# Opening an attention stream earlier in a two-block fp32 stack: buffers after the query and key projections, and 12 of 40 steps among the first fronts and value projections

## The chip, the cores and the metric

The kernel runs on one core of one Trainium2 chip. The metric is the device time of one execution in microseconds (us). TensorE is called PE here (PEld is its weight load), VectorE DVE, ScalarE ACT, and SP is the engine whose queue issues nearly all of the DMAs. Each engine works through its own list of instructions in order and waits in place when an operand or a buffer is not ready.

## What is computed

Two transformer blocks on 256 latent tokens and 256 context tokens of width 1024, all in float32. The second block has two layers, and its first layer mixes the tokens with `even_mixer`, which joins a grouped-query attention (8 heads, 2 key/value heads) with a two-directional RWKV-7 scan (8 heads):

```python
def even_mixer(h_lat, h_ctx, ...):
    p_lat = h_lat @ w_in
    p_ctx = h_ctx @ w_in
    ...
    oa_lat, oa_ctx = global_gqa(apply_rope(q_l, cos, sin), apply_rope(k_l, cos, sin), v_l,
                                q_c, k_c, v_c, ctx_out)
    f_lat = rwkv7_features(p_lat[..., A_COLS:], mu, w0, w2, a0, a2, g2, k_k, k_a)
    f_ctx = rwkv7_features(p_ctx[..., A_COLS:], mu, w0, w2, a0, a2, g2, k_k, k_a)
    ob_lat, ob_ctx = rwkv7_bidir(f_lat, f_ctx, r_k, gn_w, gn_b, ctx_out)
    o_lat = jnp.concatenate([oa_lat, ob_lat], axis=-1) @ w_out
```

The attention's result and the scan's result meet only in the output projection `w_out`. The attention needs the query and key/value projections; the scan needs the projections of r, k, v and of the decay, rate and gate vectors.

## The kernel before

Large products are split into a high and a low part and done as three matmuls (`mm3`, profile lines L113 to L115), so PE has three times the work of one product, and weights are cast on ACT (`whi`) and DVE (`wlo`) as they arrive.

`even_mixer` takes its projections and the first preparations of the scan in the order of the list `GA`: `q0` (queries), `r0` to `r3` (r and k of the scan), `k0` (keys and values of the attention), and then a mixture of `f` (the "front" of a unit of the scan), `b` (its "back"), `s` (its triangular solve) and `v0` to `v3` (the value projections). A unit of the scan is one direction of one block of 128 tokens; there are eight, numbered in the order of use. A front (L1461 on) makes the decays: `sg`, `eo`, `ei`, `ak`. A back makes `ar`, `bk` and the masked products `g` (L1540, with L1555 for the transposes), and stores a part of them to DRAM as `dq`. The solve (L1566) loads `dq` as `dl`, does 28 small DVE operations (`dt`, `dl`) one after the other, and stores `dy`. `do_k` and `do_q` store keys and queries to DRAM as `kd` and `qd`; `do_v` transposes its projection in the PSUM tag `tr` and stores it as `vd` (`stage`).

When the list is done, the pools of the projections are closed and `rwkv` begins. It goes through the units in four passes of two units each: `rwkv_maps` (products `m` with `x`, `T`, `lw`, `am`; L1609 to L1663) and then two scan steps (`rwkv_step`, products `y`, L1681 and L1690). Between the items of a pass it sets pieces of backs, solves and fronts of later units (`ahead_of`), pieces of gates and readout (`side`), and one step of the attention (`fill(FP)`, with `FP = 1`).

The attention (`even_attention`, `gqa`) is a generator of 40 steps: 8 pieces of 5 steps. The first four pieces use the first key/value head, the others the second; of each four, two have 512 keys (called big here: scores `sc` of 128x512 a head) and two have 256 (small: 128x256). The four heads of a piece each take a score (two matmuls into `sc`, L1001), a row maximum on DVE (L1003), an exponential on ACT (L1004), a reciprocal on DVE (L1005), a scaling by turns on ACT and DVE, transposes (`tr`, L1019) and a copy into `gpt`; the fifth step multiplies with the values (L1047) and stores to DRAM (`oTd`). A new piece puts two scores at its first step. The tag `sc` has one PSUM bank and so has `tr`, so that a score waits until the exponential of the one before has read its bank. Before, the generator is made at the start of `rwkv`, with a pool `at` of its own that is opened there, and its loads (`vv`, `K` of the first key/value head, `qS`) are issued at its first step; `K` has one buffer, so that the second load waits for the last score of the first four pieces.

What follows `rwkv` is `mixed`: output projection, with the stored attention output loaded as `orel`. Its first weight is `raw<-in_even_out`.

Of the kernel before, what the change touches and what calls it, by code (L numbers as in the profile page):

```python
# [45 lines left out]
def kernel(ctx: ExitStack, tc: tile.TileContext, A: dict, out: bass.AP, taps=None):  # L46
# [9 lines left out]
    def nm(s):  # L56
        uid[0] += 1
        return f"{s}_{uid[0]}"
# [58 lines left out]
    def tt(o, a, b, op):  # L117
        V.tensor_tensor(out=o, in0=a, in1=b, op=op)  # L118
# [101 lines left out]
    def acopy(d, s):  # L220
        S.copy(out=d, in_=s)
# [847 lines left out]
    def even_mixer(l, en):  # L1069
        T = 512  # L1070
        close_psum()
        with tc.tile_pool(name=nm("em"), bufs=1) as pk, tc.tile_pool(name=nm("rf"), bufs=2) as fp, \
# [59 lines left out]
            close_x()  # L1132
            held = [tc.tile_pool(name=nm("ru"), bufs=2), tc.tile_pool(name=nm("rs"), bufs=1)]
            C["up"], C["us"] = [held[0].__enter__(), None], held[1].__enter__()
            with tc.tile_pool(name=nm("ga"), bufs=1) as ga, tc.tile_pool(name=nm("emw"), bufs=2) as wk:
                zt = ga.tile([128, 260], F32, tag="zt", name="zt")
                V.memset(zt, 0.0)
                for x in dy:
                    nc.sync.dma_start(out=x.rearrange("l (a x) -> l a x", a=4), in_=zt[0:64].unsqueeze(1).to_broadcast([64, 4, 260]))
                K = ga.tile([128, 4, 512], F32R, tag="K", name="K0")  # L1140
                vv = ga.tile([128, 4, 128], F32, tag="vv", name="vv0")
                ropec = const("ropec", ga)
                rows = const("rows_g", ga)
                hsel = const("hsel", ga)
                tab = ga.tile([128, 2, 2, 2, 64], F32, tag="tab", name="tab")
                for gi in range(2):
                    g = rows[:, gi * 64:(gi + 1) * 64]
                    for t in range(2):
                        tt(tab[:, gi, t, 0], ropec[:, t, 0], g, ALU.mult)
                        g2 = g.rearrange("p (d s) -> p d s", s=2)  # L1150
                        z2 = tab[:, gi, t, 1].rearrange("p (d s) -> p d s", s=2)
                        r2 = ropec[:, t, 1].rearrange("p (d s) -> p d s", s=2)
                        for a in range(2):
                            tt(z2[:, :, a], r2[:, :, a], g2[:, :, 1 - a], ALU.mult)

                def stage(dst, n, srcs):
                    o = wk.tile([128, 4, 128], F32, tag="st", name=nm("st"), bufs=1)
                    transpose4(o[:, :n], srcs, lambda o, s: acopy(o, s.rearrange("p (j t) -> p j t", j=n)))
                    nc.sync.dma_start(out=dst, in_=o[:, :n])

                def do_k(_):
                    pss = proj_tok(A["even_kv"], 4, 256, 4, pre=())
                    for t in range(4):
                        x = wk.tile([128, 128], F32, tag="ks", name=nm("ks"))
                        y = wk.tile([128, 128], F32, tag="ky", name=nm("ky"))
                        acopy(x, pss[t][:, 0:128])
                        acopy(vv[:, t], pss[t][:, 128:256])
                        rs = head_norm(wk, x, 2, None)
                        yg, xg = (a.rearrange("p (g d) -> p g d", g=2) for a in (y, x))
                        if t < 2:  # L1170
                            rope_pairs(wk, x, 2, tab[:, 1, t, 0], tab[:, 1, t, 1], y)
                        else:
                            tt(yg, xg, rows[:, 64:128].unsqueeze(1).to_broadcast([128, 2, 64]), ALU.mult)
                        tt(yg, yg, bc(rs, 64), ALU.mult)
                        halves_of(wk, y, 2, True, K[:, :, t * 128:(t + 1) * 128])
                    nc.sync.dma_start(out=D["k"], in_=r32(K))
                    nc.sync.dma_start(out=D["vv"], in_=vv)

                def do_q(_):
                    pss = proj_tok(A["even_q"], 4, pre=preq)  # L1180
                    for t in range(4):
                        x = wk.tile([128, 512], F32, tag="qs", name=nm("qs"))
                        y = wk.tile([128, 512], F32, tag="qy", name=nm("qy"))
                        acopy(x, pss[t])
                        rs = head_norm(wk, x, 8, 0.125)
                        yg, xg = (a.rearrange("p (g d) -> p g d", g=8) for a in (y, x))
                        if t < 2:
                            rope_pairs(wk, x, 8, tab[:, 0, t, 0], tab[:, 0, t, 1], y)
                        else:
                            tt(yg, xg, rows[:, 0:64].unsqueeze(1).to_broadcast([128, 8, 64]), ALU.mult)  # L1190
                        tt(yg, yg, bc(rs, 64), ALU.mult)
                        qq = wk.tile([128, 8, 128], F32R, tag="qk", name=nm("qk"), bufs=1)
                        halves_of(wk, y, 8, False, qq)
                        nc.sync.dma_start(out=D["q"][:, t], in_=r32(qq))


                def shifted(j):
                    hi, lo = wload(A["even_r"][j])
                    ps = pst("mm")
                    for k in range(8):  # L1200
                        w = slice(k * 128, (k + 1) * 128)
                        mm3(ps, hi[:, w], lo[:, w], xh[k], xl[k], k == 0, k == 7)
                    return shift(j, ps, wk.tile([128, 512], F32, tag="rf", name=nm("rf"), bufs=3))

                def do_r(f):
                    kf = shifted(4 + f)
                    rf = shifted(f)
                    sq = wk.tile([128, 512], F32, tag="qs", name=nm("sq"))
                    S.activation(out=sq, in_=kf, func=AF.Square, scale=rc[:, 0, f:f + 1])
                    rk = wk.tile([128, 512], F32, tag="qy", name=nm("rkr"))  # L1210
                    stt(rk, rf, rc[:, 2, f:f + 1], kf, ALU.mult, ALU.mult)
                    ps = pst("fr")
                    for i, x in enumerate((sq, rk)):
                        for t in range(4):
                            c = 8 * i + 2 * t
                            E.matmul(out=ps[:, c:c + 2], lhsT=x[:, t * 128:(t + 1) * 128], rhs=hsel, start=True, stop=True)
                    vcopy(bon[:, :, 2 * f:2 * f + 2], ps[:, 8:16].rearrange("p (t a) -> p t a", t=4))
                    rs = small(8, "kkrs")
                    rsq(rs, ps[:, 0:8], 1.0, 1e-6, tag="kk")
                    ps = pst("fr")  # L1220
                    for t in range(4):
                        rb = wk.tile([128, 2, 64], F32, tag="rb", name=nm("rb"))
                        vcopy(rb, bc(rs[:, 2 * t:2 * t + 2], 64))
                        E.matmul(out=ps[:, t * 128:(t + 1) * 128], lhsT=rb.rearrange("p a b -> p (a b)"), rhs=ident, start=True, stop=True)
                    kk = wk.tile([128, 512], F32, tag="kk", name=nm("kk"), bufs=1)
                    stt(kk, kf, rc[:, 0, f:f + 1], ps, ALU.mult, ALU.mult)
                    for i, x in enumerate((rf, kf, kk)):
                        nc.sync.dma_start(out=D["f"][:, 4 * i + f], in_=x)

                units = [rwkv_in(fp, C, D, un) for un in order]  # L1230

                def front(u):
                    next(units[u])

                def back_steps(u):
                    for r in units[u]:
                        if r:
                            order[u].update(r)
                            return
                        yield  # L1240

                def back(u):
                    for _ in back_steps(u):
                        pass

                def solve(*us):
                    rwkv_solve(C, *(order[u] for u in us))

                def do_v(f):
                    vf = shifted(8 + f)  # L1250
                    stage(D["v"][:, :, f * 128:(f + 1) * 128], 4, [vf[:, t * 128:(t + 1) * 128] for t in range(4)])

                do = dict(k=do_k, q=do_q, r=do_r, v=do_v, f=front, b=back, s=solve)
# [702 lines left out]
```

## Time and profile before

| | |
|---|---|
| median of 3 runs | 2336.53 us (2333.61 to 2338.04) |
| the profiled execution's own time | 2338.83 us |
| its span in the trace | 2337.0 us (1.83 us lie around it) |
| mean granted PE clock | 0.982 |
| PE, DVE, ACT busy | 96%, 67%, 46% of the span |
| from the first value projection (889) to the first matmul of the output projection (1176.4) | 287.4 us, PE busy 252.63 us |

A granted clock of 1.00 is PE's level of 2.4 GHz, 0.50 its level of 1.2 GHz. Times inside the profile count from the start of the span. The busy time of PE counts matmuls with modelled ends.

### The profile page before, as it was taken

How to read it: one execution, taken by the hardware profiler on the slowest of the kernel's cores; microseconds unless marked ns; L12 is line 12 of the kernel's file. 1: busy time of each engine (PE TensorE's matmuls, PEld its weight loads, DVE VectorE, ACT ScalarE, POOL GpSimd, SP SyncE). 2: the span in 40 equal slices, each digit the busy share in tenths (PEclk: the TensorE clock that was granted, in tenths of full speed). 3: DMA queues.
4: the chain of work that ended last, by engine and by line, in shares of the span. 5: the costliest groups of instructions: out<-in, count | busy, mean ns of one | idle time of the engine just before them, and what ended most of it. 6: DMA issues, size and time to landing. Idle time of an engine off the chain costs nothing.

```text
span 2337.0 us, 35487 instructions
## 1 busy us (share of the span) xinstructions
PE 2250.4 (96%) x13714; PEld 1841.1 (79%) x13714; DVE 1563.4 (67%) x2993; ACT 1074.5 (46%) x1887; POOL 5.6 (0%) x10
## 2 busy tenths in 40 slices
PE   8999999999999998998889999999999999999998
PEld 6688788877787786776667778787778788768998
DVE  7867778766845768878588677437755334787555
ACT  6756666322224638765535222224422223476444
POOL 0000000000000000000000000000000000000000
PEclk9999999999999999999989999999999999999999
DMA  8556544554623535332354455323553222314553
GB/s 294 175 185 207 179 149 163 191 179 159 202 96 110 172 139 146 102 91 69 85 203 145 166 189 176 131 89 121 179 189 125 92 98 92 104 37 142 185 183 119
DMA packets 161944, 342.01 MB, mean 146 GB/s; under 512 B 48624, under 2 KB 76272, under 8 KB 161648
## 3 DMA queue, kind: packets, MB, share of 16 engines
q1 hardware_dynamic: 161056, 339.15, 43.8%
q8 instruction: 108, 1.77, 0.3%
q10 hardware_dynamic: 720, 0.60, 0.1%
q14 instruction: 60, 0.49, 0.1%
HBM read 321.86 MB, written 17.84 MB: 145 GB/s over the span
## 4 chain that ended last, share of the span: by engine, by line
PE 88%; DVE 6%; ACT 4%; DMA 2%; issue 1%; SPq 0%; DVEq 0%; ACTq 0%
PE mm L113 25%; PE mm L115 24%; PE mm L114 24%; PE m L1609 1%; PE tr L217 1%; PE m L1663 1%; DVE wlo L96 1%; PE po L1047 1%; PE wm L272 1%; PE wm L329 1%; PE gg L1540 1%; PE tr L1047 1%; ACT whi L95 1%; PE po L531 1%; PE y L1681 1%
## 5 line engine op out<-in xcount | busy, mean ns | idle before, releaser
L95 ACT CAST whi<-raw 128x1024 fp32r<-128x1024 f32 (+2 forms) x437 | 437.3, 1001 | 956.9 <-PE mm L114 587.4
L113 PE MATMUL mm<-xh,whi 128*128 128x512 f32 (+1 forms) x1912 | 679.8, 359 | 12.8 <-ACT xh L95 5.7
L115 PE MATMUL mm<-xh,wlo 128*128 128x512 f32 (+1 forms) x1912 | 679.2, 356 | 4.7 <-DVE wlo L96 4.3
L114 PE MATMUL mm<-xl,whi 128*128 128x512 f32 (+1 forms) x1912 | 679.1, 356 | 1.2 <-DVE xl L96 1.1
L96 DVE TENSOR_TENSOR wlo<-raw,whi 128x1024 fp32r<-128x1024 f32 (+2 forms) x437 | 507.9, 1164 | 249.5 <-ACT whi L95 243.1
L113 PEld LDWEIGHTS mm<-xh,whi 128*128 128x128 f32 x1912 | 363.4, 191 | 77.1 <-ACT whi L95 17.4
L115 PEld LDWEIGHTS mm<-xh,wlo 128*128 128x128 f32 x1912 | 363.9, 191 | 58.2 <-DVE wlo L96 8.4
L114 PEld LDWEIGHTS mm<-xl,whi 128*128 128x128 f32 x1912 | 364.3, 191 | 55.2 <-DVE xl L96 3.9
L115 PE MATMUL mm<-hh,wlo 128*128 128x512 f32 (+1 forms) x704 | 260.3, 370 | 0.0
L114 PE MATMUL mm<-hl,whi 128*128 128x512 f32 (+1 forms) x704 | 258.4, 367 | 0.1
L113 PE MATMUL mm<-hh,whi 128*128 128x512 f32 (+1 forms) x704 | 257.0, 366 | 0.0
L127 DVE SCALAR_TENSOR_TENSOR macc<-raw,modc,macc 128x1024 f32<-128x1024 f32 x189 | 234.9, 1280 | 0.8 <-DMA raw<-in_w_mod 0.3
L127 DVE SCALAR_TENSOR_TENSOR xres<-mm,mod,xres 128x256 f32<-128x256 f32 x216 | 96.6, 480 | 161.8 <-PE mm L115 161.4
L118 DVE TENSOR_TENSOR fg<-mm,fg 128x512 f32<-128x512 f32 (+1 forms) x84 | 52.4, 624 | 162.2 <-PE mm L115 162.1
L113 PEld LDWEIGHTS mm<-hh,whi 128*128 128x128 f32 x704 | 132.2, 188 | 27.6 <-ACT whi L95 2.5
L114 PEld LDWEIGHTS mm<-hl,whi 128*128 128x128 f32 x704 | 132.2, 188 | 26.1 <-DVE hl L96 0.7
L113 PE MATMUL mm<-whi,xh 128*128 128x512 f32 (+1 forms) x360 | 143.6, 404 | 8.9 <-ACT whi L95 8.4
L115 PEld LDWEIGHTS mm<-hh,wlo 128*128 128x128 f32 x704 | 132.5, 188 | 22.8
L114 PE MATMUL mm<-wlo,xh 128*128 128x512 f32 (+1 forms) x360 | 143.5, 399 | 2.8 <-DVE wlo L96 2.8
L115 PE MATMUL mm<-whi,xl 128*128 128x512 f32 (+1 forms) x360 | 141.9, 396 | 0.0
L113 PEld LDWEIGHTS mm<-whi,xh 128*128 128x128 f32 x360 | 68.7, 191 | 30.0 <-issue 9.2
L114 PEld LDWEIGHTS mm<-wlo,xh 128*128 128x128 f32 x360 | 69.0, 192 | 17.1 <-DVE wlo L96 5.2
(401 smaller groups left out, 2539.6 us busy)
## 6 DMA issues: line engine op xcount, KB each, us to landing
raw<-in_ffn_in SPq DMA_DIRECT2D x176, 512.0 KB, 3.5
raw<-in_w_mod SPq DMA_DIRECT2D x144, 512.0 KB, 4.5
raw<-in_ffn_out SPq DMA_DIRECT2D x64, 448.0 KB, 3.2
raw<-in_w_in_even SPq DMA_DIRECT2D x32, 512.0 KB, 4.9
raw<-in_w_in_odd SPq DMA_DIRECT2D x32, 512.0 KB, 4.1
raw<-in_ffn_out SPq DMA_DIRECT2D x32, 512.0 KB, 3.6
raw<-in_w_ple_gate SPq DMA_DIRECT2D x16, 512.0 KB, 3.7
raw<-in_even_r SPq DMA_DIRECT2D x15, 512.0 KB, 3.6
```

Source lines behind the costliest of these rows:

```text
L95: S.copy(out=hi, in_=src)
L96: V.tensor_tensor(out=lo, in0=src, in1=r32(hi), op=ALU.subtract)
L113: E.matmul(out=ps, lhsT=ah, rhs=bh, start=first, stop=False)
L114: E.matmul(out=ps, lhsT=ah, rhs=bl, start=False, stop=False)
L115: E.matmul(out=ps, lhsT=al, rhs=bh, start=False, stop=last)
L118: V.tensor_tensor(out=o, in0=a, in1=b, op=op)
L127: V.scalar_tensor_tensor(out=o, in0=a, scalar=s, in1=b, op0=op0, op1=op1)
L217: E.transpose(ps[:, j * 128:(j + 1) * 128], s, ident)
L272: E.matmul(out=ps[32 * j:32 * j + 32, hf * 256:hf * 256 + 256], lhsT=cz[:, 4 * g + j, 10 - 2 * c:42 - 2 * c], rhs=raw[:, j], start=c == 0 ...
L329: E.matmul(out=ps[32 * j:32 * j + 32], lhsT=mod_1[:, 2 - q:34 - q], rhs=acc[:, v, hf * 512:hf * 512 + 512], start=q == 0, stop=q == 2)
L531: E.matmul(out=po[:, 0:128], lhsT=pt[:, j * 128:(j + 1) * 128], rhs=vt[:, j, c], start=j == 0, stop=j == nk - 1)
L1047: E.matmul(out=po[half(a), 0:256], lhsT=vt[:, j], rhs=pt[:, j, 2 * a:2 * a + 2], start=j == 0, stop=j == nk - 1)
```

## The change

`even_mixer` closes the pools of the projections after the first six entries of `GA` (`GS = 6`, just after `k0`), opens `at` where they lay and makes the attention's generator there. A new pool `emv` holds what the value projections need (`rf` with three buffers, `st` with one). Each of the other twelve entries of `GA` is followed by as many steps of the attention as `GF` says, 12 in all. `rwkv` no longer opens `at`; its own use of the generator is as before. No operation is added or removed.

```diff
+GS = 6
+GF = (0, 1, 1, 0, 1, 1, 1, 1, 0, 2, 2, 2)
...
-            with tc.tile_pool(name=nm("ga"), bufs=1) as ga, tc.tile_pool(name=nm("emw"), bufs=2) as wk:
+            first = ExitStack()
+            ga, wk = (first.enter_context(tc.tile_pool(name=nm(n), bufs=b)) for n, b in (("ga", 1), ("emw", 2)))
+            wv = [wk]
...
-                    o = wk.tile([128, 4, 128], F32, tag="st", name=nm("st"), bufs=1)
+                o = wv[0].tile([128, 4, 128], F32, tag="st", name=nm("st"), bufs=1)
...
-                    return shift(j, ps, wk.tile([128, 512], F32, tag="rf", name=nm("rf"), bufs=3))
+                return shift(j, ps, wv[0].tile([128, 512], F32, tag="rf", name=nm("rf"), bufs=3))
...
-                for what, n in GA:
+            for what, n in GA[:GS]:
+                do[what](n)
+
+            first.close()
+            held.append(tc.tile_pool(name=nm("at"), bufs=1))
+            stream[0] = even_attention(D, held[2].__enter__(), ("sc", "tr", "tr"))
+            with tc.tile_pool(name=nm("emv"), bufs=1) as wv[0]:
+                for (what, n), fl in zip(GA[GS:], GF):
                     do[what](n)
+                    fill(fl)
...
-            with tc.tile_pool(name=nm("ru"), bufs=2) as up, tc.tile_pool(name=nm("rw"), bufs=1) as wk, tc.tile_pool(name=nm("at"), bufs=1) as ap:
-                stream[0] = even_attention(D, ap, ("sc", "tr", "tr"))
+            with tc.tile_pool(name=nm("ru"), bufs=2) as up, tc.tile_pool(name=nm("rw"), bufs=1) as wk:
```

The order of the instructions on the engines shows what moves. The first place is SP's queue, around the attention's loads (`K`, `vv`, `qS`; `kd`, `vvd` and `qd` are the stored keys, values and queries). Before:

```order
L1473 DMA wa_9273<-lod 64x128 x2
L1551 DMA dq_7263<-fe_8801 64x8x64
L1480 DMA sg_9283<-in_rwkv_w 128x512
L1551 DMA dq_7263<-fe_8801 64x8x64
L1437 DMA vv_9132<-vvd 128x512
L1445 DMA K_9134<-kd 128x1024
L1573 DMA dl_8894<-dq_7263 64x16x16
L1447 DMA qS_9136<-qd 128x512
L1447 DMA qS_9138<-qd 128x512
```

The same loads after the change:

```order
L1448 DMA vv_8637<-vvd 128x512
L1456 DMA K_8639<-kd 128x1024
L1458 DMA qS_8641<-qd 128x512
L1458 DMA qS_8643<-qd 128x512
L1562 DMA dq_7262<-g_8687 64x8x64 x2
L1491 DMA sg_8845<-in_rwkv_w 128x512
L1519 DMA fe_8877<-fd 128x12x128
L1584 DMA dl_8740<-dq_7262 64x16x16
```

They have moved from behind the second unit's `dq` (`dq_7263`) to ahead of the first unit's (`dq_7262`).

The second place is PE at the transposes of the first unit's back (`gg<-ident,fe`), which lie among the matmuls of a value projection (`mm`). Before:

```order
L1476 MATMUL fr_8769<-rwkv_wa_7242,wa_8766 128x512
L1555 MATMUL gg_8673<-ident_63,fe_8629 128x128 x4
L1555 MATMUL gh_8679<-ident_63,fe_8629 128x128 x4
L217 MATMUL tr_8976<-ident_63,rf_8971 128x128
L114 MATMUL mm_8989<-xl_76,whi_8985 128x512
```

After:

```order
L1487 MATMUL fr_8838<-rwkv_wa_7242,wa_8835 128x512
L1566 MATMUL gg_8714<-ident_63,fe_8670 128x128
L1003 MATMUL sc_8649<-K_8639,qS_8641 128x512 x2
L1566 MATMUL gg_8714<-ident_63,fe_8670 128x128 x3
L1566 MATMUL gh_8720<-ident_63,fe_8670 128x128 x4
L115 MATMUL mm_9132<-xh_75,whi_9128 128x512
```

The first score now stands here, with transposes and value projections behind it.

The third place is PE behind the last matmul of the value projections, up to the first map (`m<-x,g`). Before, the scores and the first products of the third unit's back (`gg<-ar,ak`), which the first map follows:

```order
L1491 MATMUL fr_9291<-rtri_7244,sg_9283 128x128 x4
L1001 MATMUL sc_9144<-K_9134,qS_9136 128x512 x2
L1001 MATMUL sc_9151<-K_9134,qS_9136 128x512 x2
L1019 MATMUL tr_9159<-ident_63,gp_9145 128x128 x4
L1001 MATMUL sc_9233<-K_9134,qS_9136 128x512 x2
L1540 MATMUL gg_9183<-ar_9169,ak_8791 128x128
```

After, the first rows behind the last matmul of the value projections (L219 are the value transposes, L1021 those of the attention):

```order
L1003 MATMUL sc_9098<-K_8639,qS_8643 128x512 x2
L1021 MATMUL tr_9003<-ident_63,gp_8989 128x128 x4
L219 MATMUL tr_9091<-ident_63,rf_9086 128x128 x4
L1003 MATMUL sc_9112<-K_8639,qS_8643 128x512 x2
L1021 MATMUL tr_9106<-ident_63,gp_8996 128x128 x4
L1021 MATMUL tr_9120<-ident_63,gp_9099 128x128 x4
L1003 MATMUL sc_9237<-K_8639,qS_8982 128x256 x2
L219 MATMUL tr_9162<-ident_63,rf_9157 128x128 x4
L1021 MATMUL tr_9170<-ident_63,gp_9113 128x128 x4
L1502 MATMUL fr_9456<-rtri_7244,sg_9448 128x128 x3
L1003 MATMUL sc_9244<-K_8639,qS_8982 128x256 x2
```

Two more scores follow ahead of the first map. Three scores stood between the last projection and the first map, and six do now (two big, four small); counted from `k0` on, twelve stand ahead of the first map instead of three, eight big and four small. In the passes, the attention's last step has moved from the fourth into the third, and between the last score of the first key/value head and the first of the second stand 39 rows of PE instead of 4.

## Rows read from the trace of the kernel before

**Rows 1.** The profile's page: busy time of PE, and the chain that ended last.

```profile
PE 2250.4 (96%) x13714; PEld 1841.1 (79%) x13714; DVE 1563.4 (67%) x2993; ACT 1074.5 (46%) x1887; POOL 5.6 (0%) x10
...
PE 88%; DVE 6%; ACT 4%; DMA 2%; issue 1%; SPq 0%; DVEq 0%; ACTq 0%
```

**Rows 2.** Busy time by stage, value projections to output projection (columns in the first line).

```profile
core 0: us, PE busy (x) PEld busy (x) DVE busy (x) ACT busy (x) POOL busy (x), PEclk, DMA share, GB/s
889.00:920.00 31.00, 30.93 (x197) 23.25 (x197) 24.91 (x50) 25.68 (x65) 0.00 (x0) 1.00 0.42 128
920.00:938.80 18.80, 11.12 (x52) 7.44 (x50) 16.50 (x59) 13.00 (x36) 5.39 (x6) 0.64 0.83 219
938.80:1000.00 61.20, 56.97 (x745) 46.09 (x744) 46.78 (x106) 44.65 (x106) 0.00 (x0) 0.97 0.40 102
1000.00:1062.00 62.00, 58.60 (x780) 46.96 (x779) 45.04 (x104) 38.70 (x96) 0.00 (x0) 0.92 0.32 82
1062.00:1126.50 64.50, 55.11 (x742) 43.36 (x737) 55.21 (x130) 35.04 (x63) 0.00 (x0) 0.97 0.35 92
1126.50:1161.00 34.50, 33.41 (x521) 26.98 (x520) 18.50 (x39) 17.92 (x40) 0.00 (x0) 1.00 0.18 50
1161.00:1176.40 15.40, 6.49 (x111) 5.82 (x111) 8.51 (x16) 5.74 (x11) 0.00 (x0) 0.60 0.38 110
```

**Rows 3.** Timeline of PE before the first map: start, us, instruction, [idle before].

```profile
929.35 1.22 PE L1001 MATMUL sc<-K,qS 128*128 128x512 f32 x2 [1.32 <-ACT st L221]
932.24 1.22 PE L1001 MATMUL sc<-K,qS 128*128 128x512 f32 x2 [1.67 <-ACT gp L1004]
...
935.05 1.22 PE L1001 MATMUL sc<-K,qS 128*128 128x512 f32 x2 [0.44 <-ACT gp L1004]
...
938.80 1.97 PE L1609 MATMUL m<-x,g 64*64 64x64 f32 x32
```

**Rows 4.** SP's timeline, and the landing times of all transfers on tile K.

```profile
890.96 0.33 SPq L1176 DMA_DIRECT2D kd<-K  x1
...
896.15 0.58 SPq L1159 DMA_DIRECT2D vd<-st  x1
...
DMA to landing us min/median/max: 3.8/4.0/4.9
```

**Rows 5.** PE's timeline in a value projection.

```profile
891.00 0.40 PE L115 MATMUL mm<-xh,wlo 128*128 128x512 f32 x1
891.24 0.40 PE L113 MATMUL mm<-xh,whi 128*128 128x512 f32 x1
```

**Rows 6.** PE's timeline behind the second load of K.

```profile
1047.55 0.76 PE L1001 MATMUL sc<-K,qS 128*128 128x512 f32 x2 [0.97 <-DMA K<-kd]
...
1052.21 1.97 PE L1690 MATMUL y<-si,g 128*64 128x64 f32 x32
...
1061.11 1.09 PE L1690 MATMUL y<-si,g 128*64 128x64 f32 x30 [0.81 <-ACT si L221]
```

**Rows 7.** The stretch behind the second load of K, columns as in rows 2.

```profile
1047.50:1060.00 12.50, 12.45 (x114) 8.83 (x114) 6.53 (x14) 4.70 (x15) 0.00 (x0) 0.59 0.31 66
```

**Rows 8.** DVE groups of 1062 to 1126.5: busy, mean ns, idle before.

```profile
L1003 DVE TENSOR_REDUCE s<-sc 128x1 f32<-128x512 f32 (+1 forms) x7 | 4.2, 604 | 0.6 <-PE sc L1001 0.4
...
L224 DVE COPY gpt<-tr 128x512 f32<-128x512 f32 x4 | 2.8, 688 | 1.2 <-PE tr L1019 1.2
...
L122 DVE TENSOR_SCALAR gp<-gp,s 128x512 f32<-128x512 f32 (+1 forms) x4 | 1.8, 439 | 0.0
...
L1005 DVE RECIPROCAL s<-s 128x1 f32<-128x1 f32 x8 | 1.2, 154 | 1.3 <-ACT gp L1004 1.3
```

**Rows 9.** PE groups of 1126.5 to 1161, the attention's three.

```profile
L1047 PE MATMUL tr<-gpt,vv 128*64 128x256 f32 x19 | 4.5, 398 | 0.0
...
L1019 PE MATMUL tr<-ident,gp 128*128 128x128 f32 x16 | 3.7, 294 | 0.5 <-ACT gpt L221 0.5
L1001 PE MATMUL sc<-K,qS 128*128 128x256 f32 x12 | 3.2, 337 | 0.0
```

**Rows 10.** PE's timeline at the end of the fourth pass.

```profile
1159.89 0.86 PE L1047 MATMUL tr<-gpt,vv 128*64 128x256 f32 x5
...
1170.74 1.97 PE L1690 MATMUL y<-si,g 128*64 128x64 f32 x32 [1.39 <-ACT si L221]
1176.37 0.80 PE L113 MATMUL mm<-xh,whi 128*128 128x512 f32 x1 [3.66 <-ACT whi L95]
```

More of the change, by code (lines that the diff above doesn't have):

```diff
@@ new lines, in even_mixer @@
+            ropec = const("ropec", ga)
+            rows = const("rows_g", ga)
+            hsel = const("hsel", ga)
+            tab = ga.tile([128, 2, 2, 2, 64], F32, tag="tab", name="tab")
+            for gi in range(2):
+                g = rows[:, gi * 64:(gi + 1) * 64]
+                for t in range(2):
+                    tt(tab[:, gi, t, 0], ropec[:, t, 0], g, ALU.mult)
+                    g2 = g.rearrange("p (d s) -> p d s", s=2)
+                    z2 = tab[:, gi, t, 1].rearrange("p (d s) -> p d s", s=2)
+                    r2 = ropec[:, t, 1].rearrange("p (d s) -> p d s", s=2)
+                    for a in range(2):
+                        tt(z2[:, :, a], r2[:, :, a], g2[:, :, 1 - a], ALU.mult)
@@ new lines, in stage, with do_k @@
+            def stage(dst, n, srcs):
+                o = wv[0].tile([128, 4, 128], F32, tag="st", name=nm("st"), bufs=1)
+                transpose4(o[:, :n], srcs, lambda o, s: acopy(o, s.rearrange("p (j t) -> p j t", j=n)))
+                nc.sync.dma_start(out=dst, in_=o[:, :n])
+            def do_k(_):
+                pss = proj_tok(A["even_kv"], 4, 256, 4, pre=())
+                for t in range(4):
+                    x = wk.tile([128, 128], F32, tag="ks", name=nm("ks"))
+                    y = wk.tile([128, 128], F32, tag="ky", name=nm("ky"))
+                    acopy(x, pss[t][:, 0:128])
+                    acopy(vv[:, t], pss[t][:, 128:256])
+                    rs = head_norm(wk, x, 2, None)
+                    yg, xg = (a.rearrange("p (g d) -> p g d", g=2) for a in (y, x))
+                    if t < 2:
+                        rope_pairs(wk, x, 2, tab[:, 1, t, 0], tab[:, 1, t, 1], y)
+                    else:
+                        tt(yg, xg, rows[:, 64:128].unsqueeze(1).to_broadcast([128, 2, 64]), ALU.mult)
+                    tt(yg, yg, bc(rs, 64), ALU.mult)
+                    halves_of(wk, y, 2, True, K[:, :, t * 128:(t + 1) * 128])
+                nc.sync.dma_start(out=D["k"], in_=r32(K))
+                nc.sync.dma_start(out=D["vv"], in_=vv)
@@ new lines, in do_q @@
+            def do_q(_):
+                pss = proj_tok(A["even_q"], 4, pre=preq)
+                for t in range(4):
+                    x = wk.tile([128, 512], F32, tag="qs", name=nm("qs"))
+                    y = wk.tile([128, 512], F32, tag="qy", name=nm("qy"))
+                    acopy(x, pss[t])
+                    rs = head_norm(wk, x, 8, 0.125)
+                    yg, xg = (a.rearrange("p (g d) -> p g d", g=8) for a in (y, x))
+                    if t < 2:
+                        rope_pairs(wk, x, 8, tab[:, 0, t, 0], tab[:, 0, t, 1], y)
+                    else:
+                        tt(yg, xg, rows[:, 0:64].unsqueeze(1).to_broadcast([128, 8, 64]), ALU.mult)
+                    tt(yg, yg, bc(rs, 64), ALU.mult)
+                    qq = wk.tile([128, 8, 128], F32R, tag="qk", name=nm("qk"), bufs=1)
+                    halves_of(wk, y, 8, False, qq)
+                    nc.sync.dma_start(out=D["q"][:, t], in_=r32(qq))
@@ new lines, in even_mixer, with front, back_steps, back @@
+            units = [rwkv_in(fp, C, D, un) for un in order]
+            def front(u):
+                next(units[u])
+            def back_steps(u):
+                for r in units[u]:
+                    if r:
+                        order[u].update(r)
+                        return
+                    yield
+            def back(u):
+                for _ in back_steps(u):
+                    pass
+            def solve(*us):
+                rwkv_solve(C, *(order[u] for u in us))
+            def do_v(f):
+                vf = shifted(8 + f)
+                stage(D["v"][:, :, f * 128:(f + 1) * 128], 4, [vf[:, t * 128:(t + 1) * 128] for t in range(4)])
@@ L1255, in even_mixer @@
+            do = dict(k=do_k, q=do_q, r=do_r, v=do_v, f=front, b=back, s=solve)
+            for what, n in GA[:GS]:
[5 more added lines that the diff above has]
+                for (what, n), fl in zip(GA[GS:], GF):
                     do[what](n)
+                    fill(fl)
```

137 lines of the change are left out of this document (35 added, 102 removed).

## The prediction

> **What bounds the kernel now.** I read the page first: PE is busy for 96% of the span and makes 88% of the chain that ended last [rows 1]. Work that is only moved can win where PE stands idle or runs at its lower clock. So the second view is busy time by stage from the value projections to the output projection [rows 2]: 287.4 us with 252.63 us of PE work, 34.8 us of idle PE. The reader is to see that the stages differ. In 889 to 920 PE is full (30.93 of 31, clock 1.00). In 920 to 938.8, from the projections to the first map, it works 11.12 of 18.8 us at a clock of 0.64. In the first two passes (938.8 to 1062) it is nearly full. In the third (1062 to 1126.5) it stands 9.4 us, and DVE is busy for 55.21 of 64.5 us. In the fourth (1126.5 to 1161) it is full again, and behind it lies the exposed end of the scan with 8.9 us idle. The third view is the timeline of the transition: three scores, each waiting for the exponential of the one before because `sc` has one bank, start 2.89 and 2.81 us apart, and the first map starts 3.75 us behind the third [rows 3].
>
> **The change, part by part.** The change moves nine scores, with their transposes, value products, DVE and ACT operations, from the passes to the stretch before the first map. The sum is its price there against what the passes lose.
>
> First map, a loss. (a) The first score now waits for the load of K, and the transposes and the projection's matmuls stand behind it on PE. The store of the keys is issued at 890.96, the load behind it can go when that has landed and when SP has passed the store of 896.15; transfers on this tile land 3.8 to 4.9 us after issue [rows 4]. An issue at about 897 or 898 and 4.0 us give 901.5; the place on PE where the score stands was reached at about 900 before the change. I take 1.5 us, between 0 and 4. (b) Six scores with their transposes and one value product among the projections are new work for a full PE. A 512-column matmul starts 0.24 us after the one before it [rows 5], so a score of two is 0.47 us; the five value products in a row of rows 10 take 0.86 us, which with 0.40 us for the last is 0.115 us from one to the next, and I use that for transposes as well. Six scores 2.8, some twenty transposes 2.3, eight value products of 256 columns 0.9: 6 us. The last projection ends at about 927.5 instead of 920. (c) Behind it come six scores. At the spacing of rows 3 for the two big ones, and for the four small ones about 0.6 us less (half of the columns to be multiplied, reduced and exponentiated), the sixth starts 2 x 2.85 + 3 x 2.25 = 12.5 us behind the first, and the first map 3.75 us after that: at 944 if everything else is ready. But DVE and ACT work through the same list in order: reductions, scalings and copies now stand among the small operations of the two solves, so that the second solve and the back of the third unit come late too, and the first score behind the projections also waits for an exponential. I take 948, which is +9 us; the bounds are +3 (the 6 us of (b) cost nothing) and +20 (six links of 2.85 us behind the projections are 17.1; with 7.5 of (a) and (b), less the 5.7 us between the first and third score that were there before, 19, and 21 with (a) at its 4).
>
> The 6 us of (b) rest on PE being full in 889 to 920. The trace says so twice: busy 30.93 of 31, and matmuls that start 0.24 us apart with no wait between [rows 2, 5]. The Trainium skill (Trainium Kernel Development and Optimization, section Performance Expectations) calls the matmuls' busy time a bad metric, because they are pipelined, and the busy share of the weight loads a good one. By the weight loads' 23.25 us of 31 [rows 2] there would be 7.75 us of room, and (b) would cost nothing; the first map would stand at about +3 and the sum below would be six us better. I go by the starts, and keep the other as a rival.
>
> Passes one and two, a gain of 1.6. In the first, one score of eight turns from big to small; in the second, one small score of nine goes away. A small score with all its matmuls is about 1 us of a full PE (by the starts worked out for the fourth pass), a big one about 0.6 us more.
>
> Second load of K, a gain of 3.6. Before, PE waited 0.97 us for it and then ran 12.5 us at a mean clock of 0.59: 32 products `y` took 1.97 us there against 1.09 for 30 of them once the clock was back [rows 6, 7]. With 39 rows of PE between the scores that end and start a head, instead of 4, the load is covered: 1.0. Of the 12.45 us of work at the lower clock half, 5 to 6 us, could come back if no other gap takes the clock down in its place; bounds 0 and 5.2, I take 2.6.
>
> Third pass, a gain of 5. It holds seven scores before (five big) and three small ones after. DVE's attention work there is 4.2 + 2.8 + 1.8 + 1.2 = 10.0 us [rows 8], of which three scores of half the columns keep about 3.5; so 6.5 us go from the engine that is busy for 86% of this pass [rows 2], and about as much from PE. I take 5 between 3 and 6.5.
>
> Fourth pass, a gain of 5. The attention's 47 matmuls go [rows 9]. Their busy times add up to 11.4 us but overlap; at 0.115 us from start to start for 35 of them and about 0.17 for the 12 scores it is 6.1 us. PE is busy for 33.41 of 34.5 us, so nearly all of it shortens the pass; what is left has waits of maps for DVE and ACT that the attention covered. I take 5 between 3 and 6.1.
>
> Nothing at the end: the output projection's first weight is loaded behind the last `y`, and 1176.37 keeps its distance from 1170.74 [rows 10].
>
> Sum: +9 - 1.6 - 3.6 - 5 - 5 = -6.2 us. The profiled execution, 2337.0 us of span and 1.83 around it, becomes 2338.83 - 6.2 = 2332.6; it lies 2.3 us above the median, so the median becomes 2330.3. A measurement of this kernel tells 0.2%, 4.7 us, from no change.
>
> **Rivals.** (1) No change that can be told, about 2336: work that is moved from a full PE to a full PE is worth nothing, and only the idle time counts. For it: 889 to 920 has no gap, the fourth pass hardly one, and the first map's bound of +20 cancels everything. Against it: pass three has 9.4 us of idle PE with DVE as its bound. It is the case if the first map comes 13 to 17 us later: 2334 to 2338. (2) Slower, about 2344: the chain of single-bank scores. If every link behind the projections takes the 2.85 us of rows 3, and the stalls ahead take the clock to the 0.64 of that stage for the stretch, the first map comes at 958 to 960, +20 us, and with the half-clock stretch of the second load not won back (a gain of 0 there) the sum is +20 - 1.6 - 1.0 - 5 - 5 = +7.4. For it: the transition's clock, and that `sc` and `tr` have one bank each, with the value transposes in the same `tr`. Against it: half of the links are small, and transposes and the third unit's front lie between. It decides from a first map at 956 on, where +17 less the other 12.6 is 4.7 us. (3) Much faster, about 2324: the projections have room for the scores, (b) is free, the first map comes at +3, and the sum is -12.2. For it: the weight loads' busy share [rows 2], and that a score's two matmuls bring two weight loads only. Against it: the starts 0.24 us apart. The rule of the Trainium skill named above is what speaks for it; the trace bears it out least of all.
>
> **How the numbers follow.** Forecast (2325 to 2333.5) 0.42; no change (2333.5 to 2340) 0.27; slower (2340 on) 0.18; much faster (below 2325) 0.13. Of the forecast's own range a sixth, 0.07, lies within 4.7 us of the median of before, and of the second case 0.01 on either side does not. Faster by over 0.2%: 0.42 - 0.07 + 0.13 + 0.01 = 0.49. Within: 0.07 + 0.25 = 0.32. Slower: 0.18 + 0.01 = 0.19. For 8 in 10, the range leaves out 0.07 below 2321 and 0.12 above 2342.5; the likeliest case's own range is 2325 to 2333.5.
>
> **What would show it.** A PE wait for the load of K near 901 shows (a). The end of the last projection near 927.5 shows (b), near 921 rival 3. The first map near 948 and the starts of six scores ahead of it show (c). No wait for K near the second head, and a clock of 1.00 where it was 0.59. A third pass of 59 to 60 us with DVE busy for about 49, and a fourth of 29 to 30. The forecast falls if the first map comes 15 us later, or if the passes are as long as before because another engine's chain (DVE's of maps, ACT's copies) bounds them.

## The result

| | before | after |
|---|---|---|
| median of 4 runs | 2337.28 us | 2349.94 us (2348.39 to 2351.34) |
| ratio, 95% interval | | 1.0054 (1.0038 to 1.0070) |
| profiled execution: time, span, mean granted PE clock | 2338.83, 2337.0, 0.982 | 2349.90, 2348.1, 0.983 |

The change makes the kernel 12.7 us slower; the forecast was 2330.3, in a range from 2321 to 2342.5.

Busy time by stage after the change, from 889 to the output projection, cut at the first map of each pass (columns as in [rows 2], whose own cuts lie within 0.8 us of the first maps of before, which start at 938.80, 1000.78, 1062.19 and 1126.52):

```profile
889.00:957.10 68.10, 58.92 (x337) 42.49 (x335) 51.15 (x139) 51.15 (x133) 1.52 (x2) 0.92 0.43 123
957.10:1017.50 60.40, 56.19 (x766) 44.95 (x764) 47.14 (x108) 45.18 (x109) 4.02 (x5) 1.00 0.50 128
1017.50:1075.90 58.40, 54.00 (x755) 43.47 (x754) 44.42 (x100) 36.75 (x88) 0.00 (x0) 1.00 0.30 72
1075.90:1138.60 62.70, 50.49 (x695) 42.01 (x694) 51.22 (x123) 28.50 (x52) 0.00 (x0) 0.89 0.32 83
1138.60:1185.20 46.60, 33.31 (x587) 29.21 (x585) 21.49 (x35) 17.63 (x31) 0.00 (x0) 0.87 0.24 74
```

The first three passes before the change, cut in the same way (the fourth is the last two lines of [rows 2]):

```profile
938.80:1000.80 62.00, 57.77 (x749) 46.38 (x747) 47.17 (x106) 45.09 (x107) 0.00 (x0) 0.97 0.40 101
1000.80:1062.20 61.40, 58.00 (x780) 46.80 (x779) 44.65 (x103) 38.29 (x95) 0.00 (x0) 0.92 0.32 83
1062.20:1126.50 64.30, 54.91 (x734) 43.23 (x732) 55.21 (x130) 35.00 (x62) 0.00 (x0) 0.97 0.35 92
```

The stretch ahead of the first map is 68.1 us long instead of 49.8: +18.3. The four passes, the last with the end of the scan, give back 1.6, 3.0, 1.6 and 3.3 us. That leaves +8.8 us at the output projection (1185.19 against 1176.37); another 2.3 us come behind it, where no step of the change is. The first 1.5 of them lie between 1219 and 1256 of before, where the same work ran at a granted clock of 0.93 instead of 0.96; the rest was not traced. The sum of PE's busy time is what it was, 252.91 us against 252.63 [rows 2]; its idle time is 43.3 us instead of 34.8. So the work was moved as planned, and much of the time it left behind stayed empty: in the third pass PE stands 12.2 us (9.4 before), in the fourth and the end 13.3 (10.0 before), and the third pass's clock is 0.89 instead of 0.97.

How the way to the first map looks, from the timeline of PE after the change (start, us, instruction, [idle before]); it answers to [rows 3]:

```profile
903.60 0.70 PE L1003 MATMUL sc<-K,qS 128*128 128x512 f32 x2 [2.43 <-DMA qS<-qd]
...
930.92 0.39 PE L117 MATMUL mm<-xh,wlo 128*128 128x512 f32 x1
...
933.11 0.73 PE L1003 MATMUL sc<-K,qS 128*128 128x512 f32 x2 [0.75 <-ACT gp L1006]
...
937.43 0.73 PE L1003 MATMUL sc<-K,qS 128*128 128x512 f32 x2 [1.20 <-ACT gp L1006]
...
941.61 0.78 PE L1003 MATMUL sc<-K,qS 128*128 128x256 f32 x2
...
946.52 0.77 PE L1003 MATMUL sc<-K,qS 128*128 128x256 f32 x2
...
947.65 3.16 PE L1049 MATMUL tr<-gpt,vv 128*64 128x256 f32 x16
950.74 0.50 PE L1003 MATMUL sc<-K,qS 128*128 128x256 f32 x2
...
955.08 0.51 PE L1003 MATMUL sc<-K,qS 128*128 128x256 f32 x2
...
957.14 1.15 PE L1620 MATMUL m<-x,g 64*64 64x64 f32 x32
```

The first score waits 2.43 us for `qS`; the last projection starts at 930.92, 11.5 us later than before; and the six scores behind it start 4.2 to 4.9 us apart, not 2.85 and 2.25. The score of 950.74 stands behind sixteen value products of the attention's own (947.65), which took 3.16 us at the lower clock. A part of DVE's timeline in the first of these links shows why that one is as long:

```profile
934.24 0.69 DVE L120 TENSOR_TENSOR sg<-fr,sg 128x512 f32<-128x512 f32 x1 [2.43 <-DMA sg<-in_rwkv_w]
...
935.83 0.68 DVE L1005 TENSOR_REDUCE s<-sc 128x1 f32<-128x512 f32 x1
```

The score of 933.11 is in PSUM at 933.84, but its maximum starts at 935.83: DVE waited 2.43 us for the load of another unit's `sg` and then had that operation, small operations of the solve, a reciprocal and a scaling ahead of it. SP issued this load at 929.27; `sg` has one buffer, and PE's last products with its former content had started at 928.52 and took 0.71 us. The exponential follows at 936.60, the next score at 937.43.

What the attention takes of PE before the first map, by its lines, after the change (scores, transposes, value products; here the columns are PE busy, PEld busy, clock, DMA):

```profile
889.00:957.10 68.10, 8.12 (x24) 4.24 (x24) 0.92 0.43 123
889.00:957.10 68.10, 7.31 (x38) 4.68 (x38) 0.92 0.43 123
889.00:957.10 68.10, 5.96 (x32) 2.77 (x32) 0.92 0.43 123
```

The same before the change (scores, transposes; there were no value products yet):

```profile
889.00:938.80 49.80, 3.67 (x6) 1.50 (x6) 0.86 0.58 162
889.00:938.80 49.80, 1.11 (x4) 0.71 (x4) 0.86 0.58 162
```

That is 21.4 us against 4.8. By this sum of busy times 16.6 of the 18.3 us are attention work of PE, and the idle time there did not shrink (9.2 us after, 7.75 before [rows 2]). Up to the end of the last projection it is 9.4 us of scores, transposes and value products:

```profile
889.00:931.30 42.30, 4.10 (x12) 1.95 (x12) 1.00 0.43 132
889.00:931.30 42.30, 2.48 (x16) 1.81 (x16) 1.00 0.43 132
889.00:931.30 42.30, 2.81 (x16) 1.15 (x16) 1.00 0.43 132
```

### The profile page after: what moved, and what is told of

Read it like the earlier page. It is cut to its first block, busy times and chain, and to the rows that moved or that the text cites. A ratio compares the mean times of both kernels' runs of the same rounds, so it can differ in the third digit from the quotient of the medians.

```text
span 2348.1 us, 35498 instructions
## 1 busy us (share of the span) xinstructions
PE 2251.7 (96%) x13714; PEld 1843.2 (78%) x13714; DVE 1562.8 (67%) x2993; ACT 1073.2 (46%) x1887; POOL 5.7 (0%) x10
## 4 chain that ended last, share of the span: by engine, by line
PE 87%; DVE 6%; ACT 5%; DMA 2%; issue 1%; POOL 0%; SPq 0%; POOLq 0%; DVEq 0%; ACTq 0%
PE mm L115 25%; PE mm L117 24%; PE mm L116 24%; PE m L1620 1%; PE tr L219 1%; PE m L1674 1%; PE po L1049 1%; PE wm L274 1%; PE wm L331 1%; DVE wlo L98 1%; ACT whi L97 1%; PE po L533 1%; ACT lw L223 0%; PE gg L1551 0%; PE sc L1021 0%
## 5 line engine op out<-in xcount | busy, mean ns | idle before, releaser
L115 PEld LDWEIGHTS mm<-xh,whi 128*128 128x128 f32 x1912 | 363.2, 191 | 78.4 <-ACT whi L97 17.3
```

Of the source, the lines that this page charges most:

```text
L115: E.matmul(out=ps, lhsT=ah, rhs=bh, start=first, stop=False)
```

## The experiments

Each ratio is to the kernel before in runs on the same chip, with its 95% interval. "no_fill" is the reference for most: it has the change's early pools and none of its early steps.

**The opening alone, and the two halves of the steps.**

```diff
-GF = (0, 1, 1, 0, 1, 1, 1, 1, 0, 2, 2, 2)
+GF = (0,) * 12                                    # no_fill
+GF = (0, 1, 1, 0, 1, 1, 1, 1, 0, 0, 0, 0)         # fill_fronts
+GF = (0, 0, 0, 0, 0, 0, 0, 0, 0, 2, 2, 2)         # fill_values
```

no_fill: 

> The changed kernel with all twelve fill counts at 0: the pools are opened after k0 as in the change, but the attention takes its first step in rwkv as before. Theory A (the chain: twelve scores ahead of the first map, one bank, engines in order, cost the time): the first map is back within 2 us of 938.8 and the time within 4 us of before. Theory B (the opening: the pool that lies where the projections' pools lay, and st with one buffer, cost it): still 7 us or more slower than before, with the first map at 946 or later.

fill_fronts: 

> Only the six fills among the fronts, backs and solves are kept, the six behind v1 to v3 are 0. Theory A: the wait for qS near 901 (2.4 us) stays, the projections end 6 to 9 us later than before, but only three or four scores stand behind them, so that the first map comes at 948 to 951 and the time is 3 to 7 us above before. Theory B: as the change, 11 to 13 us above before. Theory C (the loss is the wait for qS and the scores on a full PE among the projections, not the chain behind them): first map at 953 or later.

fill_values: 

> Only the six fills behind v1 to v3 are kept. Theory A: no wait near 901, the last projection near 920 as before, then eight or nine scores of which each takes 3 to 4.5 us: first map at 950 to 956, time 5 to 11 us above before. Theory C: first map near 942, time within 4 us of before.

Measured: no_fill 0.9979 (0.9969 to 0.9988), 5 us faster than before; fill_fronts 1.0026 (1.0016 to 1.0036), 6 us slower; fill_values 0.9990 (0.9981 to 0.9999), 2 us faster than before but some 2.5 slower than no_fill. Theory B is out: with the opening alone the kernel is not slower, and the first map comes at 940.5. Why it is faster is seen further down. Busy time by stage of no_fill, cut at the first maps:

```profile
889.00:940.50 51.50, 43.73 (x259) 31.88 (x258) 41.18 (x104) 39.39 (x102) 5.40 (x6) 0.87 0.61 169
940.50:1004.90 64.40, 58.85 (x743) 46.40 (x742) 46.56 (x112) 43.37 (x104) 0.00 (x0) 0.92 0.36 88
1004.90:1061.20 56.30, 53.41 (x781) 43.99 (x780) 45.56 (x104) 37.76 (x93) 0.00 (x0) 1.00 0.37 91
1061.20:1122.10 60.90, 53.57 (x726) 42.86 (x726) 54.07 (x130) 34.70 (x63) 0.00 (x0) 0.97 0.36 91
1122.10:1169.60 47.50, 37.55 (x632) 31.98 (x628) 27.79 (x56) 24.18 (x53) 0.00 (x0) 0.90 0.26 76
```

Its passes take 229.1 us (before: 237.6), with all of their attention in them; those of the change, with nine scores fewer, take 228.1. The return for nine scores is 1.0 us in these two profiles. Their price is the first map, 940.5 here and 957.1 there.

The two halves have the same attention work ahead of the first map: seven scores each, and in the trace 54 records of scores, transposes and value products among 294 and 295 of PE in all. Still the first map lies 13 us apart. In fill_fronts (first line) the first score waits 2.35 us for `qS`, the last projection starts at 932.03, and the first map at 951.7, 12.9 us later than before. In fill_values (second line) the first map comes at 938.8, as before, with PE idle for 3.5 us only and at full clock:

```profile
889.00:951.70 62.70, 55.40 (x294) 40.55 (x292) 47.42 (x122) 46.40 (x118) 1.95 (x3) 0.86 0.46 128
```

```profile
889.00:938.80 49.80, 46.26 (x295) 33.49 (x293) 43.14 (x108) 44.16 (x115) 2.60 (x3) 1.00 0.58 162
```

The 9.1 us more of busy PE in fill_fronts are not more work. From the last projection to the first map, fill_fronts (first line) ran at a clock of 0.63, as the kernel before did at 0.64 [rows 2], and fill_values (second line) at full clock:

```profile
932.40:951.70 19.30, 14.49 (x53) 9.78 (x52) 14.49 (x46) 13.74 (x37) 1.95 (x3) 0.63 0.52 132
```

```profile
924.40:938.80 14.40, 11.03 (x74) 7.03 (x74) 13.57 (x44) 13.42 (x37) 2.60 (x3) 1.00 0.68 178
```

Where the steps stand makes the difference. In fill_values four scores and eight transposes, 4.15 us of PE's busy time, lie among the projections, and the last projection starts at 923.99, 4.6 us later than before: that stretch was full. The other three scores, with sixteen transposes and a piece's value products, lie behind it, where PE stood idle before, and cost nothing there. Theory A's 950 to 956 for fill_values is missed by far, while theory C's terms (near 942, the time within 4 us) fit; in fill_fronts 951.7 lies between the two theories, and only one score stands behind its projections, so that it took no chain of scores to make the first map late. Nor do the halves add up: alone they move the first map by 12.9 us and by nothing, together by 18.3. How much of the rest is the longer chain, and how much the clock, these runs do not separate.

fill_values loses 3.7 us in its first pass instead (68.1 against 64.4) and gains nothing later (166.0 against 164.7 us). The scheduler that orders the instructions had put its first score at 904.4 as well, so that the halves aren't cleanly "early" and "late".

**Banks.** Two kernels deal the PSUM banks of the stretch after `k0` anew.

```diff
+            close_psum()
+            open_psum(mm=2, sc=2, tr=1, gg=1)             # sc_two; mm_two: sc=1
             first.close()
```

sc_two: 

> The change, with the PSUM banks of the stretch after k0 dealt anew: two banks for scores, two instead of three for projections. Theory A in its narrow form (a score waits only for its one bank): the links behind the projections fall from 4.3 us to about 3, the first map comes 5 to 8 us earlier and the time is 2342 to 2345. Rival D (the links are the sum of the operations that stand in order on DVE, ACT and PE, the bank is only where it is seen): first map within 2 us of 957, time within 3 us of the change.

mm_two: 

> Control to sc_two: the change with two banks for the projections and one for scores (one bank stands empty). If the third projection bank is what sc_two lost: as sc_two or slower, 2357 to 2362, last projection near 949. If the second bank for scores itself harms: as the change, 2348 to 2352.

Measured: sc_two 1.0092 (1.0076 to 1.0107), mm_two 1.0078 (1.0065 to 1.0091). Both lose: with two banks for projections the last of them starts at 949.07 and 947.93 instead of 930.92. Their first maps come at 960.86 and 960.60. A second bank for scores gains nothing beside that, which does not favour A in its narrow form; it does not show D either, since the two kernels have other orders than the change. What a second bank would do with three projection banks wasn't tried, since all eight are taken.

**The wait for qS.**

```diff
-            nc.sync.dma_start(out=vv, in_=D["vv"])
+            nc.gpsimd.dma_start(out=vv, in_=D["vv"])      # and the loads of K and qS
```

> The change, with the attention's loads (vv, K, qS) issued on GpSimd's queue, which holds nothing else, instead of SP's, where they stand behind a store of the values. Theory A: the first score no longer waits (2.4 us), the time falls by 2 to 3 us against the change, 10 us above before stay. Theory G (the wait at 901 delays the whole front of the change, the second unit's solve included, and is the larger part of the first map's delay): 6 us or more below the change.

Measured: 1.0044 (1.0027 to 1.0062), 2.3 us below the change by the ratios, though the intervals overlap. The first map comes at 955.28 instead of 957.14. The first score no longer waits for `qS`, but an idle time of 1.84 us that the profile puts down to its issue is left:

```profile
902.81 0.70 PE L1003 MATMUL sc<-K,qS 128*128 128x512 f32 x2 [1.84 <-issue]
```

It starts only 0.8 us earlier than in the change, the order on PE differs in places, and the last projection starts 1.2 us later (932.12). So the size agrees with theory A, but that the gain is the wait's is not shown; G is out.

**What the passes give back.** Three kernels on no_fill leave attention work out altogether, so that their outputs lack it: skip_two the first two pieces, skip_last the last two, no_attention all eight.

```diff
-                for q, nk in enumerate((4, 4, 2, 2)):
+                for q, nk in enumerate((4, 4, 2, 2)[:4 - 2 * kv]):     # skip_last
```

skip_two: 

> The kernel of no_fill (pools opened early, no fills), with the first two of the attention's eight pieces left out (8 big scores, 10 of 40 steps; their place in the output is filled with another piece's result). It is what the change would be if its ten first steps cost nothing before the first map, so it bounds what the passes can give back. By the sum of the prediction (1.6 + 5 + 5 from the passes) it is 9 to 12 us below no_fill. Theory E (the passes are bound by the chains of the maps and of the scan on DVE and ACT, and the attention only filled their gaps): at most 4 us below no_fill.

no_attention: 

> The kernel of no_fill with the attention left out altogether (its 40 steps, 32 scores; its place in the output is filled with zeros). It shows what the passes take without it. By the prediction's way of counting (PE work that leaves a pass shortens it) the passes lose some 30 us of PE work and the time falls by 25 us or more below no_fill. Theory E (the passes are bound by the chains of maps and scan on DVE and ACT, and by the clock that falls when PE waits): less than 15 us below no_fill, with more idle PE in every pass.

skip_last: 

> The kernel of no_fill with the last two of the attention's eight pieces left out (8 small scores, 10 of 40 steps), so that the first passes are as in no_fill and the fourth has hardly any attention. By the prediction's sum 5 us below no_fill for the fourth pass. Theory E: 0 to 3 us below it, and the fourth pass at 45 to 46.5 us against 47.5 from its first map to the output projection, as in the change.

Measured: skip_two 1.0015 (1.0007 to 1.0024), no_attention 0.9983 (0.9974 to 0.9992), skip_last 0.9969 (0.9959 to 0.9979), no_fill having 0.9979. Ten steps less make the kernel 8 us slower (which neither theory had) or 2 us faster, and all forty less make no difference to no_fill that the intervals would show. Busy time by stage of no_attention:

```profile
937.60:998.90 61.30, 51.15 (x675) 43.67 (x674) 37.87 (x88) 35.12 (x79) 1.20 (x2) 0.83 0.36 86
998.90:1056.80 57.90, 47.79 (x720) 40.24 (x718) 38.70 (x79) 28.38 (x65) 0.00 (x0) 0.91 0.27 63
1056.80:1118.30 61.50, 47.78 (x662) 39.99 (x660) 47.20 (x107) 21.40 (x37) 0.00 (x0) 0.86 0.30 78
1118.30:1170.20 51.90, 36.50 (x585) 32.45 (x585) 23.14 (x41) 17.50 (x33) 0.00 (x0) 0.73 0.25 73
```

Its passes are 232.6 us long, 3.5 longer than with the whole attention, and PE stands idle for 49.4 us of them. What PE waits for is seen in its timeline around the start of the fourth pass:

```profile
1112.21 1.98 PE L1695 MATMUL y<-si,g 128*64 128x64 f32 x32 [1.27 <-ACT yac L223]
1115.59 1.98 PE L1704 MATMUL y<-si,g 128*64 128x64 f32 x32 [1.40 <-ACT si L223]
1118.33 1.97 PE L1623 MATMUL m<-x,g 64*64 64x64 f32 x32 [0.76 <-DVE x L1618]
...
1123.37 0.37 PE L1623 MATMUL m<-x,g 64*64 64x64 f32 x1 [3.07 <-DMA x<-dy]
```

The products of the scan wait for ACT's copy of the one before, the maps for DVE or for a load, and many of the products themselves run at the lower clock (1.98 us for 32; at full clock it is 1.15, as for this one of no_fill):

```profile
1051.90 1.15 PE L1701 MATMUL y<-si,g 128*64 128x64 f32 x32
```

The attention stood in these waits. Since both the waits and the clock lengthen the passes of no_attention, it doesn't show by itself which of the two kept them from shrinking. Two stretches without a difference of clock do. Fourth pass, skip_last (first line; the clock is 0.89, in no_fill 0.90): all of its attention is gone, 5.6 us of PE's busy time, and it is 45.4 us long instead of 47.5; 2.1 us, where the prediction took 5. Third pass, after_k2 (second line; the change with a second buffer for K, described below; the clock is 0.97, as in no_fill): three small scores are left of seven, PE is busy for 6.7 us less and DVE for 3.0 us less, and it is as long as in no_fill, 60.9 us:

```profile
1124.10:1169.50 45.40, 31.91 (x589) 27.71 (x585) 21.84 (x37) 17.53 (x31) 0.00 (x0) 0.89 0.27 82
```

```profile
1074.90:1135.80 60.90, 46.87 (x693) 38.13 (x692) 51.02 (x123) 28.55 (x52) 0.00 (x0) 0.97 0.34 86
```

So in these two passes the attention's work was filling, and its leaving gave little or nothing back. In skip_two the clock has a part, as busy time by stage shows for its first pass, 70.2 us at 0.86 against no_fill's 64.4 at 0.92, with about as many matmuls (751 and 743); over the four passes it takes 238.0 us with ten steps less, against 229.1:

```profile
939.60:1009.80 70.20, 63.02 (x751) 49.26 (x750) 46.16 (x109) 43.88 (x108) 0.00 (x0) 0.86 0.37 92
```

**The second load of K.**

```diff
-                        K = pool.tile([128, 2, 512], F32R, tag="K", name=nm("K"))
+                        K = pool.tile([128, 2, 512], F32R, tag="K", name=nm("K"), bufs=2)
```

before_k2 (on before): 

> The kernel before with two buffers for K instead of one, so that the second load waits for no score. Theory F (no_fill gains its 5 us from the covered second load: no wait of 0.97 us and no half clock from 1047.5 to 1060): 3 to 6 us below before, clock 1.00 in that stretch. If the gain of no_fill comes from something else in the order: within 2 us of before.

no_fill_k2: 

> no_fill with two buffers for K. Theory F (no_fill and before_k2 gain the same thing, the covered second load): within 3 us of before_k2, 6 to 10 us below before. If the early opening has a gain of its own: 4 us or more below before_k2, 12 us or more below before.

after_k2 (on the change): 

> The change with two buffers for K. Its second load is covered already (no wait for it in its trace). Theory F: within 3 us of the change, 9 us or more above before. If the second buffer helps in some other way: 5 us or more below the change.

Measured: before_k2 0.9963 (0.9951 to 0.9975), no_fill_k2 0.9977 (0.9966 to 0.9987), after_k2 1.0054 (1.0039 to 1.0069). The buffer is worth 8.7 us to the kernel before, and nothing that can be told to no_fill and the change, whose order covers the load already. The stretch of [rows 7] in before_k2, at full clock:

```profile
1047.50:1060.00 12.50, 11.23 (x173) 8.26 (x172) 10.98 (x21) 6.05 (x15) 0.00 (x0) 1.00 0.39 87
```

So what no_fill gains is, as far as these runs tell, the covered load, which was a by-product of its order: 29 rows of PE stand between the two heads' scores there, 4 before. Theory F holds within the intervals; no_fill_k2 is nominally 3 us slower than before_k2, and the early opening shows no gain of its own. The passes of before_k2 take 228.4 us with all but three scores in them, those of the change 228.1 with nine fewer.

**The opposite of the change.** The attention starts three or six items later in the first pass, on before_k2.

```diff
                     for i, _ in enumerate(maps_of(p - 1)):
-                        fill(FP)
+                        fill(FP if p > 1 or i >= 3 else 0)            # k2_late3; 6: k2_late6
```

k2_late3: 

> The opposite of the change: the kernel before with two buffers for K, and the attention started three items later in the first pass, so that its last scores stand among the last products y. Theory H (in the passes the attention is what PE does while the maps and the scan wait, and it keeps the clock up, so that late steps are worth more than early ones): 2 to 6 us below before_k2, with a shorter stretch at half clock behind the last map. Rival (a late end of the attention delays the output projection): 2 us or more above before_k2.

k2_late6: 

> The same, started six items later; four scores then stand behind the last map and one piece is drained behind the last y. Theory H with its limit: 1 to 5 us above k2_late3, since the drained scores have nothing beside them. If lateness only helps: below k2_late3.

Measured: 0.9978 (0.9966 to 0.9991) and 0.9961 (0.9946 to 0.9976). Neither differs from before_k2 by more than the intervals, in either direction, and the later one, forecast as the worse, is nominally the better. Theory H is not borne out as a gain: when the attention is done inside the passes makes no difference that these runs can tell, which is some 3 to 4 us. The two kernels with the lowest ratios, before_k2 and k2_late6, beat both kernels of this study, and neither moves a step ahead of the first map.

## Why the prediction was wrong, step by step

The forecast of the span was -6.2 us and +11.1 were measured. Of the 17.3 us between them 9.3 lie at the first map, 5.7 in the passes and 2.3 behind them.

- **First map, (a).** The wait was there, at 901, for `qS` and not for K; 2.43 us against 1.5.
- **(b).** Wrong in size. The last projection came 11.5 us later; with the wait taken off 9.1 us, where 6 were worked out. The three attention lines up to it have busy times of 4.10 us for the six scores, 2.48 for the transposes and 2.81 for the value products, against 2.8, 2.3 and 0.9. The last count was short: a piece's value products are 16 records of the trace, and eight were reckoned.
- **The stretch is full.** Right, and against rival 3: 4.15 us of work there moved the last projection by 4.6 us in fill_values. The Trainium skill (Trainium Kernel Development and Optimization, section Performance Expectations) calls the weight loads' busy share a good metric for how close a kernel is to its roofline. Rival 3's estimate of room from that share, 7.75 us, is not borne out by fill_values; the starts of the matmuls, 0.24 us apart [rows 5], told that there was none.
- **(c).** Wrong in size, and the largest miss at the first map: what lies behind the last projection grew by 6.8 us, where 1.5 were taken. The links are 4.2 to 4.9 us long, since a score in line also waits behind other units' operations on DVE, behind the transposes that share `tr`, and once behind value products. The first map came at 957, not 948. That is rival 2's place (958 to 960). The chain on top of the other work that it named is seen in the trace, but sc_two didn't show that the single bank makes it, and the lower clock held only from about 940 to 951 (0.54 there). Rival 2's sum was +7.4, because it too let the passes return 12.6 us (and +17 less these is 4.4, not 4.7).
- **What (c) overlooked.** It priced every score behind the projections as a link. In fill_values three stood there at no cost, where PE had been idle at a clock of 0.64 before: the price depends on where each step stands.
- **Passes one and two, second load of K.** The passes lost 1.6 and 3.0 us against 5.2 forecast, and the load was covered, at full clock, as forecast. Only, this needed no early step: no_fill and before_k2 have it too.
- **Third and fourth pass.** This is the step that failed as a mechanism. "so 6.5 us go from the engine that is busy for 86% of this pass" and "so nearly all of it shortens the pass" gave 10 us; the change got 1.6 and 3.3, and no_fill, with the attention in them, had 3.4 and 2.4 of these anyway. A busy DVE and a full PE were taken for bounds. At an equal clock the third pass is 60.9 us long with seven scores and with three, and the fourth loses 2.1 us when all of its attention leaves; the attention had filled waits of the maps and the scan.
- **Nothing at the end.** The term behind the passes was put at nothing and measured +2.3 us; 1.5 of them came with a lower clock, and why the clock fell at other places there stays open.
- **Rival 1** had the right principle, that only idle time counts, but still let the passes return what had left them. The sum that holds is +18.3 for the first map, -9.5 for the passes, +2.3 behind: +11.1 of span.

## What to carry to other kernels

Work that fills another chain's waits makes an engine look full; whether the stage shrinks when the work leaves is not told by busy shares, but by a kernel that leaves the work out, read at an equal clock, and it is the first run to make before moving a filler. Moved into a stretch where the engine is the bound, a filler costs its whole time (4.15 us of work moved the last projection by 4.6); behind that stretch, where the engine stood idle, as many steps were free. Look first for a single wait with a lower clock behind it: one more buffer for one tile was worth more here (8.7 us) than any place tried for the steps.

## What was unexpected of the hardware

Less work can make PE slower. With all attention left out, the granted clock of the four passes was 0.83, 0.91, 0.86 and 0.73, against 0.92, 1.00, 0.97 and 0.90 in no_fill; nine of the twelve full blocks of 32 products `y` took 1.98 us there, two of twelve in no_fill, and the others 1.10 to 1.15. With ten steps left out, skip_two's passes were 8.9 us longer. What the clock took in each kernel varied with the order of the instructions, by up to the size of the effects looked for, so that differences of 2 or 3 us between the totals of single kernels here are not put down to a cause.
